# A layer on one core: the transfer queue from the end of attention on, in the program's order

## Chip, core and metric

The kernel runs on one core of a Trainium2 chip. The metric is the device time of one execution in microseconds (us); the profile is one more execution, taken apart by the hardware profiler. A core has TensorE (PE), VectorE (DVE), ScalarE (ACT), GpSimd (POOL) and SyncE (SP). SP computes nothing: it issues the DMA transfers, one after the other, and waits for semaphores in between.

## The reference

One encoder layer on 512 tokens of width 1024, in float32.

```python
h = rmsnorm(x, g_mix_pre)
aq, ..., gate_logits = split(h @ w_in)
ya = dsa_attention(...) @ w_up_a             # sparse attention, 8 heads
yb = stick_breaking_attention(...) @ w_up_b  # 8 heads
yc = memory_attention(...) @ w_up_c          # 4 heads on 256 memory tokens
gates = sigmoid(gate_logits + b_gate)        # three gates of (512, 1024)
merged = gates[0] * ya + gates[1] * yb + gates[2] * yc
x = x + rmsnorm(merged @ w_out, g_mix_post)
h = rmsnorm(x, g_ffn_pre)
gu = h @ w_ffn_in                            # 1024 -> 2 * 2816
x = x + rmsnorm((silu(gu[:2816]) * gu[2816:]) @ w_ffn_out, g_ffn_post)
```

## The kernel before

Every float32 product is made of three passes on TensorE. Each operand is split into a rounded high part, made by ACT (`split`, line 76), and the low rest, made by DVE (line 77); the passes are high x high, high x low and low x high. So each weight tile of 128 x 1024 floats (512 KB) goes through four steps: SP loads it (`load`, line 97), ACT casts it, DVE subtracts, TensorE uses it.

Buffers have tags, each with a fixed number. `load` puts weights into `wraw` (3 buffers) and, from the end of attention on, into `lraw` (2 buffers) for every second load. The split of a `wraw` tile goes to `wh` and `wl` (2 each), that of an `lraw` tile to a wide tile `w2` (4). `act` (22 buffers) holds nearly all else: queries, keys, merged activations, gains, and some raw weights. `h` (8) holds the normed activations, `fin` (4) the residual stream.

The order of instructions: TensorE's is the program's everywhere, by a region of `manual_schedule` around the whole layer. DVE, ACT and POOL have such regions in two places only (the first norm, and the end of mix_out). Elsewhere a scheduler orders ACT, DVE, POOL and SP ahead of time, along an estimated clock: it takes what is ready in its own plan, and prefers what stands earlier in the program. An instruction that first writes a tile can only be placed when the plan has a buffer for the tile, and the tiles of one tag are handed out in the program's order. Within a region an engine's instructions keep the order of the program; where they fall among instructions from outside the region stays the scheduler's. When the program runs, each engine goes through its list in order and waits for semaphores only.

`run` (from line 267) is the layer. What matters here comes after the attention branches:

- **merge(1)** (line 697) runs in TensorE's gaps of the last attention branch and then alone: for each of 8 column blocks a gate (weights of w_in) and an up-projection (w_up_b, 12 matmuls of 512 columns). TensorE's result is multiplied with the gate on DVE (line 726), added to `acc` on POOL (line 727), and split into a pair mT[j] of tag `act` on ACT and DVE (line 730).
- **mix_out** (line 800): the gain of the norm (`grow`, line 734, tag `act`), the four x rows (line 354, tag `fin`), then `tok_pair` (line 737) twice, for tokens 0 to 255 and 256 to 511: mT times w_out, row block after row block (12 matmuls each, line 751). In the first pass the weights of ffn blocks 0 and 1 are loaded on the way, raw into `act`; the second pass keeps four of the eight row blocks from the first.
- **ffn** (line 1001): ffn blocks 0 to 2 as plain products, and blocks 3 to 21 (`seven`, `left_sides`) by Strassen's scheme, seven products a block. A block loads its gate half into `wraw` and its up half into `lraw`.
- **ffn_out** (line 1048): the gain of the last norm (tag `h`), ten row blocks of w_ffn_out as plain products, and the other twelve by Strassen, with the products in the order 5, 1, 2, 6, 3, 7, 4. Their raw weights are read in `units51` and `unit`; some are summed by accumulating transfers from POOL (line 1070). Then the norm and the stores (line 792).

In program order the transfers of mix_out are: gain; x rows 0 to 3; w_out 0 (`wraw`), 1 (`lraw`); both halves of ffn block 0 (`act`); w_out 2, 3; both halves of block 1; w_out 4 to 7; in the second pass w_out 0, 1, both halves of block 2, w_out 2, 3. Even rows go to `wraw`, odd ones to `lraw`.

Of the kernel before, what the change touches and what calls it, by code (L numbers as in the profile page):

```python
# [48 lines left out]
class Layer:  # L49
# [217 lines left out]
    def run(self):  # L267
        w_in, w_kv = self.a["w_in"], self.a["w_mem_kv"]
        late = ExitStack()
        att = ExitStack()  # L270
        self.att = att.enter_context(self.tc.tile_pool(name="att", bufs=1))
        with self.tc.manual_schedule(engines={mybir.EngineType.PE}):
            self.setup()
            memT, mk, mv, cq = [], {}, {}, {}
            self.index_keys(cq)
            xs = [self.load_rows(self.a["mem"], t) for t in range(2)]
            for x in xs:
                self.norm_in(x)

            self.iq = {}  # L280
            iqs = lambda js: self.feat_tiles(w_in[:, C_IQ:C_IQ + 512], self.hT, self.iq, js, T - P, P,
                                             lambda ps: self.evac_q(ps[:, 0:T - P], T - P), self.w_iq)
            cqs = lambda js: self.feat_tiles(w_in[:, C_CQ:C_CQ + 512], self.hT, cq, js)
            mks = lambda js: self.feat_tiles(w_kv[:, 0:512], memT, mk, js, n=M)
            mvs = self.tok_tiles(w_kv[:, 512:1024], memT, (0, 1), mv)
            memTs = self.mem_T(xs, memT)
            iq = self.add(iqs(range(4)))
            kv = self.add(cqs((1,)), self.mix(memTs, cqs((2,)), 2), mks(range(4)), cqs((3,)), mvs)
            self.drain(iq)
            self.scores()  # L290
            self.drain(kv)
            a, aq = self.qkv(C_AQ, C_AK, C_AV)
            self.branch_c(cq, mk, mv)
            self.acc = {}
            self.add(self.merge(2, self.outC, "w_up_c"))
            self.drain(aq)
            self.select()
            self.fill(FM)
            b, bq = self.qkv(C_BQ, C_BK, C_BV)
            self.branch_a(*a)  # L300
            self.drain(bq)
            self.add(self.merge(0, self.outA, "w_up_a"))
            self.outB = []
            self.add(self.merge(1, self.outB, "w_up_b"))
            self.branch_b(*b)
            self.drain()
            att.close()
            self.late = late.enter_context(self.tc.tile_pool(name="late", bufs=1))
            self.mix_out()
            self.ffn()  # L310
        late.close()

    def setup(self):
# [687 lines left out]
    def ffn(self):  # L1001
# [31 lines left out]
        for j, u in enumerate(first[1:], 1):  # L1033
            run(products(*u, 1))
            self.gated(u[0], out(j))
# [199 lines left out]
```

## Time and profile before

| | us |
|---|---|
| median of 3 runs | 908.74 |
| lowest and highest | 907.76, 911.09 |
| profiled execution | 906.76 |
| its span, first to last instruction | 905.0 |

Busy shares of the span: TensorE 97%, DVE 75%, ACT 53%, POOL 13%. The span falls into attention with merge(1) (to about 503 us), mix_out (to about 543), the ffn blocks (to about 777) and ffn_out (to the end). A busy TensorE means matmuls in a row; the idle time in between is where a wait shows.

### The profile page before, as it was taken

Reading aid. Unit: us, or ns where it says so; the run is one execution under the profiler, and the core shown is the slowest. Engines: PE = TensorE matmul, PEld = TensorE weight load, DVE = VectorE, ACT = ScalarE, POOL = GpSimd, SP = SyncE. Lnnn points to the kernel's source line nnn. Section 1 sums busy time; section 2 is a strip of 40 time slices with the busy share of each in tenths; the row PEclk is TensorE's granted clock in tenths of the full one; section 3 lists DMA queues with packets and bytes.
Section 4 is the critical chain, followed back from the end, with each engine's and each line's share of the span. In section 5 each row is a group of like instructions: output and inputs, shape, how many; then the busy total and the mean of one; then the engine's idle time right before and its main releaser. Section 6 shows DMA issues by size and latency. Waiting matters only on the chain.

```text
span 905.0 us, 13554 instructions
## 1 busy us (share of the span) xinstructions
PE 881.1 (97%) x5110; PEld 773.9 (86%) x5110; DVE 681.5 (75%) x1174; ACT 476.0 (53%) x830; POOL 120.4 (13%) x157
## 2 busy tenths in 40 slices
PE   8999999999999999999999999999999999999995
PEld 7888888888888888888788888999999999887884
DVE  6589999953598976777563579688888887862886
ACT  6464675332666666665453454355555555542452
POOL 2000000020032303443222101500000000000101
PEclk9999999999999999999999999999999999999998
DMA  6523543443354433222384723113434334672622
GB/s 204 170 85 119 166 115 94 127 129 111 101 160 119 128 82 93 70 59 59 116 253 132 237 79 105 48 44 98 116 95 116 96 115 121 189 215 81 176 34 93
DMA packets 134341, 107.47 MB, mean 119 GB/s; under 512 B 4844, under 2 KB 115484, under 8 KB 134276
## 3 DMA queue, kind: packets, MB, share of 16 engines
q1 hardware_dynamic: 132052, 102.41, 38.5%
q0 software_dynamic: 1632, 3.15, 2.2%
q8 instruction: 40, 0.66, 0.3%
q10 hardware_dynamic: 592, 1.05, 0.3%
q14 instruction: 25, 0.20, 0.1%
HBM read 100.02 MB, written 2.12 MB: 113 GB/s over the span
## 4 chain that ended last, share of the span: by engine, by line
PE 77%; DVE 12%; issue 4%; DMA 3%; ACT 2%; POOL 1%; POOLq 0%; DVEq 0%; ACTq 0%
PE bank L88 21%; PE bank L87 21%; PE bank L89 21%; DVE wl L77 4%; PE bank L751 3%; PE bank L551 2%; PE bank L566 1%; PE bank L181 1%; PE bank L180 1%; PE bank L211 1%; DMA lraw<-in_w_ffn_out_dram 1%; PE bank L213 1%; PE bank L212 1%; DVE act L77 1%; DVE e L638 1%
## 5 line engine op out<-in xcount | busy, mean ns | idle before, releaser
L77 DVE TENSOR_TENSOR wl<-wraw,wh 128x1024 fp32r<-128x1024 f32 (+1 forms) x107 | 122.4, 1146 | 66.7 <-ACT wh L76 66.4
L76 ACT CAST wh<-wraw 128x1024 fp32r<-128x1024 f32 (+1 forms) x107 | 102.0, 955 | 111.5 <-PE bank L88 75.6
L87 PE MATMUL bank<-h,wh 128*128 128x512 f32 (+1 forms) x376 | 148.8, 396 | 0.0
L89 PE MATMUL bank<-h,wl 128*128 128x512 f32 (+1 forms) x376 | 145.3, 386 | 1.0 <-DVE wl L77 0.9
L88 PE MATMUL bank<-h,wh 128*128 128x512 f32 (+1 forms) x376 | 145.0, 386 | 0.0
L89 PEld LDWEIGHTS bank<-h,wl 128*128 128x128 f32 x376 | 70.6, 188 | 15.8 <-DVE wl L77 1.7
L87 PEld LDWEIGHTS bank<-h,wh 128*128 128x128 f32 x376 | 70.9, 189 | 11.7 <-issue 0.2
L88 PEld LDWEIGHTS bank<-h,wh 128*128 128x128 f32 x376 | 70.8, 188 | 11.5
L87 PE MATMUL bank<-act,wh 128*128 128x256 f32 (+1 forms) x204 | 69.2, 339 | 1.2 <-DVE s L976 1.2
L88 PE MATMUL bank<-act,wh 128*128 128x256 f32 (+1 forms) x204 | 68.0, 333 | 0.0
L89 PE MATMUL bank<-act,w 128*128 128x256 f32 x228 | 64.1, 281 | 0.0
L87 PE MATMUL bank<-h,w 128*128 128x256 f32 x228 | 64.1, 281 | 0.0
L88 PE MATMUL bank<-h,w 128*128 128x256 f32 x228 | 64.1, 281 | 0.0
L89 PE MATMUL bank<-h,w 128*128 128x256 f32 x228 | 64.1, 281 | 0.0
L87 PE MATMUL bank<-act,w 128*128 128x256 f32 x228 | 64.1, 281 | 0.0
L88 PE MATMUL bank<-act,w 128*128 128x256 f32 x228 | 64.1, 281 | 0.0
L615 POOL TENSOR_TENSOR p<-toep,score 128x128 f32<-128x128 f32 (+3 forms) x32 | 30.5, 967 | 200.2 <-DVE score L524 102.9
L77 DVE TENSOR_TENSOR act<-act 128x512 fp32r<-128x512 f32 (+1 forms) x47 | 36.0, 778 | 22.3 <-ACT act L76 22.2
L76 ACT CAST act<-act 128x512 fp32r<-128x512 f32 (+1 forms) x47 | 31.6, 692 | 32.6 <-POOL act L727 13.9
L77 DVE TENSOR_TENSOR w<-wl,w 128x1024 fp32r<-128x1024 f32 x38 | 46.3, 1218 | 1.5 <-ACT w L76 1.0
L87 PE MATMUL bank<-h,act 128*128 128x256 f32 (+2 forms) x152 | 46.8, 308 | 0.0
L88 PE MATMUL bank<-h,act 128*128 128x256 f32 (+2 forms) x152 | 45.7, 301 | 1.1 <-DVE h L81 1.1
(224 smaller groups left out, 2306.4 us busy)
## 6 DMA issues: line engine op xcount, KB each, us to landing
wraw<-in_w_in_dram SPq DMA_DIRECT2D x64, 512.0 KB, 3.7
lraw<-in_w_ffn_in_dram SPq DMA_DIRECT2D x20, 512.0 KB, 3.9
wraw<-in_w_ffn_in_dram SPq DMA_DIRECT2D x20, 512.0 KB, 3.7
wraw<-in_w_ffn_out_dram SPq DMA_DIRECT2D x13, 512.0 KB, 4.5
lraw<-in_w_ffn_out_dram SPq DMA_DIRECT2D x12, 512.0 KB, 3.6
wraw<-in_w_mem_kv_dram SPq DMA_DIRECT2D x8, 512.0 KB, 3.9
lraw<-in_w_out_dram SPq DMA_DIRECT2D x6, 512.0 KB, 6.1
wraw<-in_w_out_dram SPq DMA_DIRECT2D x6, 512.0 KB, 4.6
```

The source lines that it names most:

```text
L76: self.nc.scalar.copy(hi, src)
L77: (eng or self.nc.vector).tensor_tensor(lo, src, hi.bitcast(F32), op=OP.subtract)
L87: self.nc.tensor.matmul(out, lhsT=sh, rhs=mh, start=first and i == 0, stop=False, **kw)
L88: self.nc.tensor.matmul(out, lhsT=sh, rhs=ml, start=False, stop=False, **kw)
L89: self.nc.tensor.matmul(out, lhsT=sl, rhs=mh, start=False, stop=last and i == n - 1, **kw)
L180: self.nc.tensor.matmul(out, lhsT=x, rhs=y[:, 0:n], start=True, stop=False)
L181: self.nc.tensor.matmul(out, lhsT=x, rhs=y[:, T:T + n], start=False, stop=True)
L211: self.nc.tensor.matmul(ps, lhsT=ah[:, s], rhs=wh[:, k2], start=st, stop=False)
L212: self.nc.tensor.matmul(ps, lhsT=ah[:, s], rhs=wl[:, k2], start=False, stop=False)
L551: self.nc.tensor.transpose(ps[:, c:c + P], p[i][:, j * P:(j + 1) * P], self.ident)
L615: nc.gpsimd.tensor_tensor(s, toep[0][:, 0:n][:, ::-1], self.mask[i], op=OP.add)
L751: self.nc.tensor.matmul(ps[c], lhsT=st_[:, s], rhs=mv_[:, 0, c * 512:(c + 1) * 512], start=f and k == order[0], stop=l and k == order[-1])
```

## The change

`run` wraps its last two calls in a region in which SP, too, issues in the order of the program:

```diff
             self.late = late.enter_context(self.tc.tile_pool(name="late", bufs=1))
-            self.mix_out()
-            self.ffn()
+            with self.tc.manual_schedule(engines={mybir.EngineType.SP}):
+                self.mix_out()
+                self.ffn()
         late.close()
```

`ffn` calls `ffn_out`, so all transfers from the gain of mix_out to the last store on SP are in the region. The loads of merge(1) are not. The transfers that ACT and POOL issue stay as they are.

## Rows read from the trace of the kernel before

**Rows 1.** The page, part 1: busy us (share of the span) x instructions, by engine.

```profile
PE 881.1 (97%) x5110; PEld 773.9 (86%) x5110; DVE 681.5 (75%) x1174; ACT 476.0 (53%) x830; POOL 120.4 (13%) x157
```

**Rows 2.** Busy time by stretch: length, engines, TensorE's granted clock, DMA share, GB/s.

```profile
450.00:460.00 10.00, 10.00 (x46) 8.28 (x45) 4.43 (x5) 3.79 (x7) 1.67 (x1) 1.00 0.98 355
505.00:525.00 20.00, 20.00 (x89) 16.28 (x88) 10.41 (x10) 8.32 (x10) 2.14 (x1) 1.00 0.83 262
530.00:575.00 45.00, 42.11 (x278) 37.78 (x277) 37.15 (x74) 22.24 (x48) 8.83 (x10) 1.00 0.36 106
760.00:780.00 20.00, 18.75 (x157) 18.50 (x156) 16.57 (x26) 13.01 (x20) 1.37 (x1) 1.00 0.49 144
800.00:830.00 30.00, 28.52 (x123) 22.72 (x122) 16.55 (x19) 13.12 (x17) 1.21 (x1) 1.00 0.59 176
```

**Rows 3.** TensorE's timeline, end of merge(1) and last matmul: start, us, instruction.

```profile
503.13 0.39 PE L89 MATMUL bank<-act,wl 128*128 128x512 f32 x1
...
504.09 0.73 PE L751 MATMUL bank<-wl,act 128*128 128x512 f32 x2
...
894.00 0.40 PE L89 MATMUL bank<-w,act 128*128 128x512 f32 x1
```

**Rows 4.** SP's timeline, end of attention to mix_out (x2, x3: two, three transfers).

```profile
447.75 1.29 SPq L354 DMA_DIRECT2D fin<-in_x_dram  x3
...
454.31 0.90 SPq L97 DMA_DIRECT2D lraw<-in_w_out_dram  x2
...
483.91 2.29 SPq L97 DMA_DIRECT2D wraw<-in_w_up_b_dram  x2
492.07 12.32 SPq L97 DMA_DIRECT2D wraw<-in_w_out_dram  x4
504.44 0.43 SPq L734 DMA_DIRECT2D act<-in_g_mix_post_dram  x1
```

**Rows 5.** Timelines of DVE and of ACT around the end of merge(1).

```profile
490.81 1.23 DVE L77 TENSOR_TENSOR wl<-wraw,wh 128x1024 fp32r<-128x1024 f32 x1 [2.49 <-ACT wh L76]
492.68 0.69 DVE L726 TENSOR_TENSOR gate<-bank,gate 128x512 f32<-128x512 f32 x1 [0.64 <-PE bank L89]
...
504.56 0.68 DVE L726 TENSOR_TENSOR gate<-bank,gate 128x512 f32<-128x512 f32 x1
...
495.14 0.62 ACT L76 CAST act<-act 128x512 fp32r<-128x512 f32 x1 [2.07 <-POOL act L727]
...
500.61 1.05 ACT L76 CAST wh<-wraw 128x1024 fp32r<-128x1024 f32 x1 [1.51 <-PE bank L88]
...
507.56 0.62 ACT L76 CAST act<-act 128x512 fp32r<-128x512 f32 x1 [3.00 <-POOL act L727]
508.08 1.05 ACT L76 CAST wh<-wraw 128x1024 fp32r<-128x1024 f32 x1
```

**Rows 6.** Busy time by stretch behind the last matmul; the clock is the seventh figure.

```profile
897.00:898.00 1.00, 0.00 (x0) 0.00 (x0) 0.16 (x1) 0.92 (x3) 0.00 (x0) 0.83 0.96 367
898.00:900.00 2.00, 0.00 (x0) 0.00 (x0) 1.52 (x5) 0.42 (x2) 0.93 (x1) 0.50 0.01 2
```

**Rows 7.** SP's timeline at the end of the ffn blocks.

```profile
742.30 0.34 SPq L97 DMA_DIRECT2D wraw<-in_w_ffn_out_dram  x1
...
762.14 0.34 SPq L97 DMA_DIRECT2D wraw<-in_w_ffn_out_dram  x1
765.88 0.33 SPq L734 DMA_DIRECT2D h<-in_g_ffn_post_dram  x1
766.30 6.62 SPq L97 DMA_DIRECT2D lraw<-in_w_ffn_out_dram  x2
```

**Rows 8.** Timelines of DVE and of ACT at the start of ffn_out.

```profile
771.34 1.22 DVE L1135 TENSOR_TENSOR act<-wraw,lraw 128x1024 f32<-128x1024 f32 x1 [0.66 <-DMA lraw<-in_w_ffn_out_dram]
...
799.59 1.23 DVE L1135 TENSOR_TENSOR act<-wraw,lraw 128x1024 f32<-128x1024 f32 x1 [4.95 <-DMA lraw<-in_w_ffn_out_dram]
...
774.66 1.05 ACT L76 CAST wh<-wraw 128x1024 fp32r<-128x1024 f32 x1
```

## The prediction

> **What bounds the kernel now.** I read the page first, then busy time by stretch, then SP's timeline, then TensorE, VectorE (DVE), ScalarE (ACT) and GpSimd (POOL) around the place where the change begins. TensorE is busy for 97% of the span [rows 1]; in the part that the change reaches it is full in 450 to 460 and in 505 to 525, and misses 2.89 us in 530 to 575, 1.25 us in 760 to 780 and 1.48 us in 800 to 830 [rows 2]. Add the tail behind the last matmul (it starts at 894.00 and takes 0.40, [rows 3]; the span is 905.0): some 5.6 us of holes and 10.6 us of tail are all that a better order could win. Transfers don't bound it: 0.83 of the DMA engines' time in 505 to 525, and 0.98 in 450 to 460, with TensorE full in both [rows 2]. What can cost is a hole put into TensorE's stream, whose order is fixed by hand.
>
> **What SP does now.** At the end of attention the scheduler runs ahead of the program. The x rows leave at 447.75, and while merge(1) (gates and up-projection, ends at 503.5) still runs, the odd rows of w_out leave from 454.31 on, through the `lraw` buffers that nothing else wants [rows 4]. The even rows wait for a `wraw` buffer from merge(1): four of them from 492.07 on. The first transfer of mix_out in the program, the gain row, leaves at 504.44, behind 14 later ones [rows 4]. It has nothing to wait for in the data: it goes into an `act` buffer. Tiles of one tag are handed out in the program's order, and the `act` tiles just ahead of it are the eight pairs mT that merge(1) writes. So in the scheduler's plan the gain can't get its buffer before ACT takes up the split of mT[7], though at run time a buffer has been free for long. That is the hinge of this case.
>
> **The change, part by part.** It adds and removes no instruction. From mix_out on it chains SP's list: gain, four x rows, w_out 0, 1, two halves of ffn block 0, w_out 2, 3, block 1, w_out 4 to 7, and so on; in ffn_out the gain of the last norm, and then w_ffn_out.
>
> 1. *The plan.* The gain is now the head of the chain, and all 14 transfers that the plan used to place ahead of it (four x rows, nine w_out rows, one half of ffn block 2) are behind it. In the plan the first w_out row therefore starts after the split of mT[7] is begun, and its conversion (ACT `wh`, then DVE `wl`) must stand behind that split in ACT's queue. Before, the conversion of w_out 0 stood at 500.61, ahead of the splits of mT[6] and of mT[7] (507.56) [rows 5].
>
> 2. *The run.* SP only follows semaphores, and there it is not late: behind the last up-projection load (by 483.91 + 2.29 = 486.2, [rows 4]) the gain and the x rows go out at once, w_out 0 goes when its `wraw` buffer is free, at about 492.07 as now, and w_out 1 just behind it. The five early transfers are 2.6 MB; at the 355 GB/s of [rows 2] that is 7.4 us, done by about 494, and w_out 0 lands by 498. Nobody uses it before 503.5. If that cover were gone, the price would be the rest of those 7.4 us.
>
> 3. *The hole.* The data are there, but ACT's queue now says mT[7] first. The last matmul of merge(1) starts at 503.13 and takes 0.39 [rows 3]: it ends at 503.52. DVE has the low half of mT[6] to do first (0.6), so its product with the gate starts at about 504.2. From that product to the split on ACT it is 2.46 us two tiles earlier (492.68 to 495.14, the POOL add in it) and 3.00 for the last tile (504.56 to 507.56) [rows 5]; DVE is emptier then, so I take 2.5: 506.7. The next conversion starts 0.52 later (507.56 to 508.08) and takes 1.05 (the one at 500.61): 508.3. There TensorE gets its first two matmuls of mix_out; the third needs `wl`, 1.23 us on DVE (490.81) [rows 5]: 509.5. That matmul starts at 504.09 now [rows 3]. Sum: 509.5 - 504.1 = **+5.4 us**. Ends: DVE's product directly at 503.56, 2.46 and the same three steps, 508.8, +4.7; DVE and POOL no quicker than now, 507.56 + 0.52 + 1.05 + 1.23 = 510.4, +6.3.
>
> 4. *What comes behind it.* Four odd rows that were converted during merge(1) are converted now while TensorE uses them: 4 x 1.23 us more on DVE, on top of 10.41 of 20 us in 505 to 525 [rows 2], makes 15.3; ACT 8.32 + 4 x 1.05 = 12.5. A row is ready every 1.23 us and TensorE needs 12 matmuls for one, 12 x 0.23 = 2.8 us (89 matmuls in 20 us, [rows 2]), so it is hidden after the first; without that cover each row would cost up to 1.2 us. SP itself is held: the last half of block 1 goes into a buffer that TensorE frees half way through merge(1)'s last 12 matmuls (12 x 0.23 before 503.5, so about 502), and w_out 4 to 7 are queued behind it, so w_out 4 leaves some 3 us later than now. It is wanted at about 520. w_out 5 and 7 wait for `lraw` buffers until w_out 1 and 3 are converted, at about 511 and 515, and are wanted at 523 and 528. Cost: 0.
>
> 5. *The clock.* After the last matmul of the kernel (ends at 894.40) the granted clock is 0.83 in 897 to 898 and 0.50 from 898 on [rows 6]: 1.2 GHz in place of 2.4 after an idle time shorter than the hole of 4.8 us in step 3. No row shows a clock that comes back. Bounds: 0, if it doesn't fall, and one step of 12 matmuls at half speed, 2.8 us. I take +1.0, nearer to none since the hole is barely longer than what it took to fall. The Trainium skill, "TensorE: Matmul & The Clock Gate" (the part on the HAM clock gate), says that low is the resting state and that only sustained matmul activity releases it. The fall at the end of this trace agrees with it; by that rule the hole would cost the slow step too, which is the second rival below.
>
> 6. *The ffn blocks.* The halves of a block now alternate strictly, where the plan had the `wraw` half one block ahead. The `lraw` half decides how far ahead a block can be loaded, it has two buffers, and it leaves when it does now; the `wraw` half then leaves just behind it, a block or more ahead of its use. Cost: 0.
>
> 7. *ffn_out.* Its gain wants an `h` buffer, free at 765.88; w_ffn_out 0 leaves at 742.30 today, and the fourth at 762.14 [rows 7]. All of them go behind the gain now. The first is converted only at 774.66 (it lacks a `wh` buffer until then, [rows 8]); leaving at 766.2, with the 5.0 us that the load at 766.30 takes to its use at 771.34 [rows 7, 8], it is there at about 771: 3 us to spare. The pair for the first Strassen sum comes some 5 us later, and DVE has waits that take this up (4.95 us at 799.59, [rows 8]). Cost 0; bounds -1.25 (the hole in 760 to 780 closes) to +5 (that wait of 4.95 lands on TensorE).
>
> 8. *The end.* Three reads of T[7] wait for `act` buffers that the first of the seven products (order 5, 1, 2, 6, 3, 7, 4) frees, and six reads that ran earlier now follow them. The first three of the six are wanted for the fifth product, the others for the seventh, and a product is 36 matmuls of 0.23, 8.3 us: 0, bounds -1 to +1. The stores keep their order.
>
> Sum: 5.4 + 1.0 = +6.4 us. The profiled execution took 906.76 us (span 905.0 and 1.8 around it), which is 2.0 under the median of 908.74; against its own time that is 913.2, and against the median 915.1.
>
> **The rivals.** *No hole*: the change doesn't do what I read into it, that is, ACT's queue keeps w_out 0 ahead of mT[7]. For it: the data are early at run time. Against it: the gain's place at 504.44, 57 us behind its successors [rows 4]. It gives 908.7. *A slow restart*: the clock falls in the hole and stays at 1.2 GHz for two steps, 5.5 us in place of 1.0: 908.7 + 5.4 + 5.5 = 919.7. *Starved ffn_out*: the list begins 24 us later (742.30 to 766.2), and the wait of DVE for a transfer at 799.59 grows to one of TensorE: 5 to 6 us more, 921. For it: 1.48 us are lost right there already; against it: the 3 us to spare in step 7 and the buffers that hold the list back anyway. *Faster*: loads in order of use close the three holes (2.89 + 1.25 + 1.48 = 5.6 us): 903.1. It decides only if there is no hole at the start of mix_out, and the holes in 530 to 575 lie in the norms between TensorE and DVE, not at a transfer.
>
> **How the numbers follow.** Forecast 0.62, no hole 0.14, slow restart 0.10, starved ffn_out 0.08, faster 0.06. The forecast's own range is +4.7 - 1.0 to +6.3 + 2.8: 912.4 to 917.8. The range has to reach the slow restart and most of the no-hole and starved cases: 909 to 921. A measurement of this kernel can tell about 0.5% (4.5 us) from no change: faster takes the last rival but for its weaker half, 0.05; same the no-hole case and the low end of the forecast, 0.18; slower 0.77.
>
> **What would show it.** In the profile after: SP's gain and x rows behind the last up-projection load, at about 486; no `lraw` load of w_out before 492; on ACT the split of mT[7] ahead of the first `wh` of w_out; a hole on TensorE of 4 to 5 us from 503.5 on, ended by ACT `wh`, and a shorter one ended by DVE `wl`; a granted clock under 1.00 in 505 to 515 if step 5 counts. The first w_ffn_out load at or behind the gain of the last norm, and holes after 760 of the size that they have now. I am wrong if TensorE runs through at 503 to 510, or if the time is lost where transfers are waited for.

## The result, and the profile after

The changed kernel takes 919.75 us (median of 4 executions, 918.88 to 920.12), the kernel before 908.25 beside it (4 executions). The ratio is 1.0124, with a 95% interval of 1.0109 to 1.0139: 11.5 us slower. The forecast was 915.1, +6.4. The sign and the first place were right; the size was not, and two more places had been put at nothing.

The profiled execution took 920.12 us, its span is 918.3, so the span grew by 13.3; that is more than 11.5 because the profiled execution before (906.76) lies under its median and this one over its own. All numbers below are places in these two spans; line numbers of the changed kernel are higher by one. First the page, part 1 (busy us, share, instructions), which answers to [rows 1]:

```profile
PE 884.7 (96%) x5110; PEld 775.8 (84%) x5110; DVE 678.6 (74%) x1174; ACT 475.5 (52%) x830; POOL 119.7 (13%) x157
```

The work is the same, instruction by instruction. TensorE is busy 3.6 us longer for the same 5110 matmuls, so some of them ran slower; the rest of the growth is idle time. Where it is idle, the view of TensorE's waits from 500 us on shows (engine and line, what was waited for, total us, times, longest):

```profile
PE bank L752 <- ACT wh L76: 4.5, 1, 4.5
PE bank L87 <- DVE s L977: 2.9, 1, 2.9
```

Before, the first of these waits did not exist and the second was 1.25 us.

**First place, the start of mix_out.** SP's timeline (start, us, instruction), to hold beside [rows 4]:

```profile
484.09 2.29 SPq L97 DMA_DIRECT2D wraw<-in_w_up_b_dram  x2
486.44 0.50 SPq L735 DMA_DIRECT2D act<-in_g_mix_post_dram  x1
487.02 2.00 SPq L355 DMA_DIRECT2D fin<-in_x_dram  x4
492.25 0.33 SPq L97 DMA_DIRECT2D wraw<-in_w_out_dram  x1
492.62 0.43 SPq L97 DMA_DIRECT2D lraw<-in_w_out_dram  x1
```

SP is early: gain and x rows right behind the last up-projection load, w_out 0 at 492.25 as before. The hole is made elsewhere. TensorE, then ACT, then DVE, to hold beside [rows 3, 5]:

```profile
503.31 0.39 PE L89 MATMUL bank<-act,wl 128*128 128x512 f32 x1
508.17 1.22 PE L752 MATMUL bank<-wh,act 128*128 128x512 f32 x2 [4.47 <-ACT wh L76]
509.43 1.22 PE L752 MATMUL bank<-wl,act 128*128 128x512 f32 x2
...
513.79 0.63 PE L752 MATMUL bank<-w,act 128*128 128x512 f32 x2
...
506.55 0.62 ACT L76 CAST act<-act 128x512 fp32r<-128x512 f32 x1 [2.76 <-POOL act L728]
507.07 1.04 ACT L76 CAST wh<-wraw 128x1024 fp32r<-128x1024 f32 x1
...
504.43 0.68 DVE L727 TENSOR_TENSOR gate<-bank,gate 128x512 f32<-128x512 f32 x1
...
508.14 1.23 DVE L77 TENSOR_TENSOR wl<-wraw,wh 128x1024 fp32r<-128x1024 f32 x1 [0.25 <-ACT wh L76]
```

ACT splits mT[7] at 506.55 and converts w_out 0 only behind it, at 507.07; before, that conversion stood at 500.61. The third matmul of mix_out starts at 509.43, before at 504.09. The matmuls of w_out 1, which start at 513.79 here, started before at

```profile
506.49 2.93 PE L751 MATMUL bank<-w,act 128*128 128x512 f32 x12
```

The next view shows the granted clock (third figure from the right; the second is TensorE's busy time):

```profile
506.00:507.00 1.00, 0.00 (x0) 0.00 (x0) 0.00 (x0) 0.45 (x1) 0.52 (x1) 0.94 1.23 321
507.00:513.00 6.00, 4.80 (x10) 3.31 (x11) 5.55 (x6) 6.00 (x8) 0.00 (x0) 0.50 0.44 142
513.00:514.00 1.00, 1.00 (x4) 0.84 (x3) 1.00 (x2) 1.00 (x2) 0.00 (x0) 0.65 0.99 356
514.00:515.00 1.00, 1.00 (x6) 0.80 (x5) 1.00 (x2) 1.00 (x2) 0.00 (x0) 1.00 0.84 344
```

The clock falls to 0.50 (1.2 in place of 2.4 GHz) at about 506.9, while TensorE is idle, and is back at about 513.7. The first w_out row is used at half speed: from the third matmul to the group with w_out 1 it is 4.36 us, before 2.40. The Trainium skill, "TensorE: Matmul & The Clock Gate" (the HAM clock gate), says that low is the resting state and matmul activity releases it; these rows agree: it is back after TensorE has worked from 508.17 on.

**Second place, the start of ffn_out.** TensorE, ACT, DVE and SP in turn:

```profile
786.42 0.39 PE L87 MATMUL bank<-act,wh 128*128 128x256 f32 x1 [2.94 <-DVE s L977]
...
782.26 1.05 ACT L76 CAST h<-wraw 128x1024 fp32r<-128x1024 f32 x1 [2.58 <-DMA wraw<-in_w_ffn_out_dram]
783.22 1.03 ACT L76 CAST wh<-wraw 128x1024 fp32r<-128x1024 f32 x1
784.94 0.63 ACT L974 ACTIVATE silu<-silu 128x512 f32<-128x512 f32 x1 [0.69 <-DVE silu L973]
...
783.35 1.23 DVE L77 TENSOR_TENSOR h<-wraw,h 128x1024 fp32r<-128x1024 f32 x1 [2.23 <-ACT h L76]
784.49 0.42 DVE L973 TENSOR_TENSOR silu<-bank,s 128x256 f32<-128x256 f32 x1
...
785.95 0.42 DVE L977 TENSOR_TENSOR s<-bank,s 128x256 f32<-128x256 f32 x1
...
772.58 0.34 SPq L735 DMA_DIRECT2D h<-in_g_ffn_post_dram  x1
772.97 0.42 SPq L97 DMA_DIRECT2D wraw<-in_w_ffn_out_dram  x1
```

The gain of the last norm leaves at 772.58 and all of w_ffn_out behind it. ACT comes to a conversion of w_ffn_out (into `h`) and stands there 2.58 us for its transfer; DVE stands 2.23 us for ACT. Behind these stands what TensorE waits for: the sum into `s` (line 977), which frees the PSUM bank (the place of TensorE's result) that the last product needs.

The tile is the first of Strassen's product 1 (`right(1, 0, ...)` in `units51`): third of w_ffn_out in the program, so third in the chain. It is one of five loads that leave within 2.6 us (SP's timeline has it at 773.92), and could be used only 8.3 us later, at 782.26. ACT had this conversion ahead of the last silu in the kernel before too, with its load there; what ended its wait then was TensorE:

```profile
766.19 1.05 ACT L76 CAST h<-wraw 128x1024 fp32r<-128x1024 f32 x1 [1.50 <-PE bank L89]
...
776.54 0.63 ACT L973 ACTIVATE silu<-silu 128x512 f32<-128x512 f32 x1 [0.83 <-DVE silu L972]
```

So it is not the order on ACT that is new here, but the late load in it. Behind this hole the clock was at 0.50 too, from about 786.8 to 790.2:

```profile
787.00:790.00 3.00, 3.00 (x13) 2.81 (x13) 2.32 (x5) 1.93 (x2) 0.00 (x0) 0.50 0.46 128
```

**Third place, the tail.** SP, DVE and TensorE:

```profile
851.40 3.11 SPq L97 DMA_DIRECT2D act<-in_w_ffn_out_dram  x3
854.62 0.41 SPq L97 DMA_DIRECT2D wraw<-in_w_ffn_out_dram  x1
...
869.51 0.37 SPq L97 DMA_DIRECT2D lraw<-in_w_ffn_out_dram  x1
...
904.48 0.68 DVE L1184 TENSOR_TENSOR act<-bank,act 128x512 f32<-128x512 f32 x1
...
909.66 0.68 DVE L1184 TENSOR_TENSOR act<-bank,act 128x512 f32<-128x512 f32 x1
...
904.08 0.40 PE L89 MATMUL bank<-w,act 128*128 128x512 f32 x1
```

The three reads of T[7] wait for `act` buffers until 851.40, and the last six reads now stand behind them (854.62 to 869.51). Before, five of the six had left by 840, ahead of T[7] at 842.10, and the last at 845.71. Their conversions reach DVE late; from 881.86 on it works almost without a break, the norms of the first two blocks of tokens come later too (to 904.0, before to 889.5), and the sum that opens the norm of the third block runs at 904.48, behind the start of TensorE's last matmul. Before it ran 2.9 us ahead of it. T[7] and that sum in the kernel before:

```profile
842.10 3.11 SPq L97 DMA_DIRECT2D act<-in_w_ffn_out_dram  x3
...
891.12 0.68 DVE L1183 TENSOR_TENSOR act<-bank,act 128x512 f32<-128x512 f32 x1
```

From one such sum to the next it is 5.2 us (904.48 to 909.66). So two of these steps follow the last matmul, where before 1.9 us of the first were left behind it (894.40 to 896.30) and the whole second: 3.3 us more.

**The account**, by where the same instruction starts in the two spans:

| where | lag, us | added there |
|---|---|---|
| last matmul of merge(1): 503.13, 503.31 | 0.18 | 0.18 |
| third matmul of mix_out: 504.09, 509.43 | 5.34 | 5.16, the hole |
| first group with w_out 1: 506.49, 513.79 | 7.30 | 1.96, the clock |
| end of the ffn blocks: 776.78, 783.48 | 6.70 | -0.60, in the norms |
| next matmul: 778.03, 786.42 | 8.39 | 1.69, second hole |
| clock at 1.00 again: 780.73, 790.64 | 9.91 | 1.52, the clock |
| last matmul: 894.00, 904.08 | 10.08 | 0.17 |
| end of the span: 905.0, 918.3 | 13.30 | 3.22, the tail |

### The profile page after: what moved, and what is told of

Read it like the earlier page. It is cut to its first block, busy times and chain, and to the rows that moved or that the text cites. A ratio compares the mean times of both kernels' runs of the same rounds, so it can differ in the third digit from the quotient of the medians.

```text
span 918.3 us, 13534 instructions
## 1 busy us (share of the span) xinstructions
PE 884.7 (96%) x5110; PEld 775.8 (84%) x5110; DVE 678.6 (74%) x1174; ACT 475.5 (52%) x830; POOL 119.7 (13%) x157
## 3 DMA queue, kind: packets, MB, share of 16 engines
HBM read 100.02 MB, written 2.12 MB: 111 GB/s over the span
## 4 chain that ended last, share of the span: by engine, by line
PE 79%; DVE 11%; issue 4%; DMA 2%; ACT 2%; POOL 2%; SPq 0%; POOLq 0%; DVEq 0%; ACTq 0%
PE bank L87 22%; PE bank L88 22%; PE bank L89 22%; PE bank L752 3%; DVE wl L77 3%; PE bank L552 2%; PE bank L567 1%; PE bank L181 1%; PE bank L180 1%; PE bank L211 1%; PE bank L213 1%; PE bank L212 1%; DVE e L639 1%; POOL rs L247 1%; DMA wraw<-in_w_ffn_out_dram 1%
## 5 line engine op out<-in xcount | busy, mean ns | idle before, releaser
L87 PEld LDWEIGHTS bank<-h,wh 128*128 128x128 f32 x376 | 70.9, 189 | 11.6 <-issue 0.2
L88 PEld LDWEIGHTS bank<-h,wh 128*128 128x128 f32 x376 | 70.8, 188 | 11.5
L89 PE MATMUL bank<-act,wl 128*128 128x512 f32 (+1 forms) x128 | 46.5, 363 | 0.0
```

The lines of the kernel that those rows point to most:

```text
L87: self.nc.tensor.matmul(out, lhsT=sh, rhs=mh, start=first and i == 0, stop=False, **kw)
L88: self.nc.tensor.matmul(out, lhsT=sh, rhs=ml, start=False, stop=False, **kw)
L89: self.nc.tensor.matmul(out, lhsT=sl, rhs=mh, start=False, stop=last and i == n - 1, **kw)
```

## Experiments

The theory: three places, each with its own cause: the first from the order that a chain on SP forces on the plan, the other two from loads that are late because of what stands ahead of them in the chain. The rivals: one cause that the later losses follow from; the program's order as such; slow matmuls for another reason than the clock.

**One part alone.** First the region over ffn alone, then over mix_out alone:

```diff
-            with self.tc.manual_schedule(engines={mybir.EngineType.SP}):
-                self.mix_out()
-                self.ffn()
+            self.mix_out()
+            self.ffn()
...
+        chain = ExitStack()
+        chain.enter_context(self.tc.manual_schedule(engines={mybir.EngineType.SP}))
         self.gated(pss, out(0))
...
         self.ffn_out(fT)
+        chain.close()
```

> SP's list is in the program's order only from the end of the norms on (ffn blocks and ffn_out); mix_out keeps the scheduler's order. Theory (the loss is a sum of places that don't depend on each other: hole of 5.2 and slow clock of 2.0 at the start of mix_out, hole of 1.7 and slow clock of 1.5 at the start of ffn_out, 3.2 in the tail): here the first two are gone and the others stay, some 6.5 us over before (914 to 915.5), and TensorE starts on mix_out at about 504 as before. Rival (what is lost in ffn_out is a consequence of the late start of mix_out, or of where the gain of mix_out stands): within 1.5 us of before.

Measured: 913.07 beside 908.09 (ratio 1.0060, 1.0039 to 1.0080), 5.0 us, a little under what was expected.

```profile
779.57 0.39 PE L87 MATMUL bank<-act,wh 128*128 128x256 f32 x1 [2.46 <-DVE s L976]
```

The second hole is there (2.46 us) and the long tail (895.52 to 909.8, 14.3 us; before 11.0). In this trace the clock stayed at 1.00 behind this hole, which is the missing 1.5 us. It is the fastest of the four executions (mean granted clock 0.995); the others have 0.988 to 0.992, so some of them hold slow clock that no trace shows.

> SP's list is in the program's order only over mix_out up to its norms; the ffn blocks and ffn_out keep the scheduler's order. Theory of separate places: a hole of about 4.5 us at 503.5 ended by ACT wh, the clock at 0.50 behind it, and nothing lost behind 780: some 6.6 us over before (914 to 915.5), and this run and the one with the region over ffn alone add up to the loss of the change, 11 to 13 us. Rival (the two parts act on each other: the queue of ffn pulls the buffers of mix_out): the sum of the two differs from the loss of the change by over 2 us.

Here the region ends ahead of mix_out's ordered tail. Measured: 915.88 (1.0079, 1.0059 to 1.0100), 7.8 us, a little over what was expected. The hole of 4.47 us and the slow clock are there; at the start of ffn_out TensorE waits 2.03 us, 0.8 more than before, and the tail is 11.2 us. The trace also has a clock of 0.50 from 555.0 to 558.4, behind a wait of 2.14 us in the norms; the kernel before waits 2.24 us there and its clock stays. The two parts add up to 12.8 us, the whole is 11.5: separate places, within the spread of the runs.

**The head of the chain.** The first gain is asked for ahead of the region:

```diff
+            self.gp = self.grow("g_mix_post", "act")
             with self.tc.manual_schedule(engines={mybir.EngineType.SP}):
...
-        gp = self.grow("g_mix_post", "act")
+        gp = self.gp
```

> As the change, but the first gain row is asked for ahead of the region, so that it isn't the head of SP's chain; all else in program order. Theory (the hole comes from the head of the chain: its act buffer is handed out behind the split of mT[7], so everything chained behind it is planned behind it too): x rows and w_out 0 are planned earlier, w_out 0 is converted ahead of mT[7]'s split, no hole over 1 us at 503.5, clock 1.00 through 505 to 515: 7 us under the changed kernel, 912 to 913.5. Rival (order itself: in program order the loads come too late or too close together, whatever the head): the hole stays within 1 us of 4.5, time within 1 us of the changed kernel.

Measured: 914.22, 5.5 us under the changed kernel where 7 were expected. ACT, then TensorE:

```profile
500.65 1.05 ACT L76 CAST wh<-wraw 128x1024 fp32r<-128x1024 f32 x1 [1.32 <-PE bank L88]
...
506.74 2.52 ACT L76 CAST act<-act 128x512 fp32r<-128x512 f32 x3 [3.09 <-POOL act L729]
...
510.26 0.73 PE L753 MATMUL bank<-wh,act 128*128 128x512 f32 x2 [0.80 <-ACT wh L76]
511.90 0.50 PE L753 MATMUL bank<-wl,act 128*128 128x512 f32 x1 [0.91 <-DVE wl L77]
```

w_out 0 is converted at 500.65, ahead of mT[7]'s split (in the group at 506.74), as before; the hole of 4.5 us is gone and the clock is at 1.00 there. What stays is 1.7 us of waits: the third row (510.26, 511.90) is converted behind that split now. That is the part of the 7 us that did not come. The wait of 2.39 us at the start of ffn_out, with the clock at 0.50 behind it, and the tail of 14.2 us are still there. So the hole is what the head of the chain had made, not program order itself.

**The buffer.** The gain stays the head of the chain, in a buffer of its own:

```diff
-    BUFS = dict(h=8, act=22, wraw=3, wh=2, wl=2, lraw=2, pt=3, fin=4)
+    BUFS = dict(h=8, act=21, wraw=3, wh=2, wl=2, lraw=2, pt=3, fin=4, gain=1)
...
-        gp = self.grow("g_mix_post", "act")
+        gp = self.grow("g_mix_post", "gain")
```

> As the change, with the first gain still the head of SP's chain, but in a buffer of its own; act has 21 buffers in place of 22, which may cost a little anywhere. Theory (what holds the chain back in the plan is the act buffer that is handed out only behind the last pair mT): with no such buffer to wait for, w_out 0 is converted ahead of mT[7]'s split and the hole of 4.5 us is gone, as with the gain ahead of the region: 912 to 915, what the 21 buffers cost included. Rival (being behind a head in program order is what counts, whatever its buffer): the hole stays within 1 us of 4.5, some 919 to 921.

The place answers: no hole, with the same two short waits behind it. ACT and TensorE:

```profile
502.61 1.05 ACT L76 CAST wh<-wraw 128x1024 fp32r<-128x1024 f32 x1 [1.39 <-PE bank L88]
...
505.13 0.39 PE L89 MATMUL bank<-act,wl 128*128 128x512 f32 x1
505.36 0.61 PE L752 MATMUL bank<-wh,act 128*128 128x512 f32 x2
```

w_out 0 is converted at 502.61, ahead of mT[7]'s split, which is in the group of ACT that starts at 508.71. So being the head alone does not make the hole; it is the `act` buffer, handed out behind the eight pairs mT. One thing stays argued: `act` has 21 buffers here, and no run has 21 with the gain still among them. The time, 918.06, is no proof of it: merge(1) ends 1.8 us later with 21 buffers, and TensorE loses 4.5 us ahead of 870, where ACT stands at conversions into `h` for three late loads in turn (4.60, 1.45 and 1.94 us), and the clock falls behind that.

**The last gain.** It is asked for where the reads of the third product follow, late in ffn_out:

```diff
-        gp = self.grow("g_ffn_post", "h")
...
         s1 = copied(px)
+        gp = self.grow("g_ffn_post", "h")
         more(3)
```

> As the change, but the gain row of the last norm is asked for where it is first needed less early, behind the ten plain row blocks of ffn_out's weights, so that the loads of w_ffn_out aren't chained behind its h buffer. Theory (the hole at the start of ffn_out is the late start of w_ffn_out's list, held by that gain): the first w_ffn_out loads leave tens of us earlier, the DVE wait of 2.9 us at 786 and the slow clock behind it are gone, 1.7 to 3.2 us under the changed kernel (916.5 to 918); the tail stays 13.8. Rival (the hole is the order of the reads themselves or of the buffers wraw and lraw): within 1 us of the changed kernel and the hole stays.

Measured: 918.42, only 1.3 us under the changed kernel. The mechanism is as expected, the gain smaller:

```profile
753.17 0.57 SPq L97 DMA_DIRECT2D wraw<-in_w_ffn_out_dram  x1
...
783.21 0.39 PE L87 MATMUL bank<-act,wh 128*128 128x256 f32 x1 [0.57 <-DVE s L977]
```

The first load leaves at 753.17 in place of 772.97, the hole is 0.57 in place of 2.94 us, and no slow clock follows. So it is the place of that gain in the chain that made the load late. Some of it comes back as waits of 0.7 and 0.5 us for ACT and 0.9 for a `wl` that were not there or shorter. The tail stays, 14.2 us. Behind the first hole the clock of this trace was low for half as long as in the changed kernel (508.5 to 511.9), which no edit here accounts for.

**T[7].** Its three reads are taken out of the chain:

```diff
+        self.chain.close()
         for i in range(n):
             T[7, i] = read(0, 1, i, "act")
             plus(T[7, i], 1, 1, i)
+        self.chain.enter_context(self.tc.manual_schedule(engines={mybir.EngineType.SP}))
```

> As the change, but the three reads of T[7] in ffn_out are taken out of SP's chain: the reads chained behind them no longer wait for the act buffers that T[7] needs. Theory (the tail of 14.2 us in place of 11.0 is the late start of six reads behind T[7], which pushes DVE's sums into the last product): those reads leave before T[7] as in the kernel before, DVE has a gap ahead of the last product, the tail is 11 us and the time 3.2 us under the changed kernel (916 to 917). Rival (the tail is longer because the whole of ffn_out starts later or because the last transfers collide): the tail stays at 14 us.

Measured: 919.89, no gain. Yet five of the six reads leave ahead of T[7] again (826.31 to 852.88, T[7] from 854.99), and the tail is 10.2 us (906.89 to 917.1). Most of the 4 us are lost again ahead of it. ACT and TensorE:

```profile
833.17 1.04 ACT L76 CAST h<-wraw 128x1024 fp32r<-128x1024 f32 x1 [6.26 <-DMA wraw<-in_w_ffn_out_dram]
834.12 1.04 ACT L76 CAST wh<-lraw 128x1024 fp32r<-128x1024 f32 x1
...
835.21 0.65 PE L87 MATMUL bank<-wh,act 128*128 128x512 f32 x1 [3.28 <-ACT wh L76]
...
906.89 0.40 PE L89 MATMUL bank<-w,act 128*128 128x512 f32 x1
```

It is the second place's mechanism again: in ACT's list a conversion whose load is late stands ahead of the one that TensorE wants, and the clock falls behind the hole. Here this order is new: the changed kernel has no conversion into `h` at that place. The tail's cause is shown: it is 14.2 to 14.3 us in six traces with T[7] in the chain (12.8 in the seventh, whose TensorE lost 4.5 us late), and 10.2 to 11.6 in the four with T[7] out of it. Taken away alone, it gave nothing back.

**Both of ffn_out's repairs.**

> As the change, with the last gain asked for later and T[7]'s reads out of SP's chain, both at once; the first gain stays the head of the chain. Theory (the hole of 3.3 us at 832 that came with freeing T[7] alone is ACT in its planned order standing at a conversion whose load is late because the whole list of w_ffn_out is late; with the list early it is at most 1.3 us, as with all three taken back): hole and slow clock at 503 to 515 stay, nothing else is lost, tail 10 to 11.2: 914 to 916.5, within 1.5 us of the run that has program order over mix_out alone. Rival (the two repairs get in each other's way, or a hole at 832 is the price of freeing T[7]): 917 or more, with a hole over 2.5 us behind 800.

Measured: 917.38 (914.22 to 918.30). The traced execution is the fastest of the four: 914.22, waits of 0.57 at 783 and 1.30 at 830, tail 11.5 us. The holes are as small as the theory said, but the clock is at 0.50 from 832.6 to 836.0 behind the waits of 1.30 and 0.76 us, the tail is a little longer than expected, and the median is 1 us above. What the other three lost isn't in a trace.

**All three taken back.**

> As the change, with three things taken back: the first gain asked for ahead of the region, the last gain asked for later, T[7]'s reads out of the chain. Theory (these three are the whole loss; program order itself costs next to nothing): hole, both slow-clock stretches and the long tail are gone; what stays are some 1.7 us of short waits for w_out rows at 509 to 512, as in the run with the first gain ahead alone: 908 to 911, within 3 us of the kernel before. Rival (something else of the order costs too): over 912.

Measured: 912.89 as the median of ten, from 908.12 to 915.87. The traced one is the fastest, 908.12: no hole at 503, short waits of 0.8 and 0.9 at 510 to 512, 0.6 at 779, 1.3 at 826, tail 11.1 us, clock at 1.00 to the last matmul. That is what was expected, but the median is 2 us over the upper end, as the rival had it: 4.9 us over the kernel before (ratio 1.0050, 1.0029 to 1.0071). The ten differ by their mean granted clock: 0.997 at 908.12, 0.992 to 0.993 at 912.4 to 912.9, 0.989 to 0.990 at 915.6 to 915.9. A step of 0.008 of some 910 us is 7.3 us; the times differ by 7.8. So the other executions hold slow clock that this trace doesn't show; behind which waits, is open.

**ffn alone, mended.** The region over ffn alone with both of ffn_out's repairs:

> Program order on SP only from the end of the norms on, with the last gain asked for later and T[7]'s reads out of the chain; mix_out has the scheduler's order. Theory (nothing is left of the loss, and the loads of ffn_out in order of use may take back the waits of 1.25 us at 777 and 1.48 us at 800 to 830): 906 to 908.5, at or up to 2 us under the kernel before. Rival (order of use does nothing for these waits, which are DVE's and ACT's own): within 1 us of before; or a new wait is made, over 910.

Measured: 911.16 (1.0038, 1.0023 to 1.0054), slower than before. The wait at 777 is 1.0 in place of 1.25 us, those in 800 to 830 grew from 1.48 to 1.90: ACT stood 4.13 us for the load of a conversion into `h` ahead of the `wh` that TensorE wanted. The clock fell twice in this trace: behind the wait of 2.12 us in the norms, ahead of the region, and behind 1.15 and 0.76 us at 826. Order of use wins nothing there. No kernel tried here is faster than the one before.

**The clock alone.** Idle transposes of the identity fill the hole:

```diff
+        idle = self.bank()
+        for _ in range(21):
+            nc.tensor.transpose(idle[:, 0:P], self.ident, self.ident)
         gp = self.grow("g_mix_post", "act")
```

> As the change, plus 21 transposes of the identity on TensorE at the start of mix_out that nobody reads, so that TensorE isn't idle through the whole hole. Theory (the slow first step behind the hole is the granted clock that falls in it): the hole for the data stays (the first matmul of mix_out at about 508), the clock is 1.00 over 505 to 515, 2 us under the changed kernel (917 to 918.5). Rival (the step is slow because its weights come late, and the clock is only a bystander): time and the start of the second step unchanged, within 0.7 us.

Measured: 917.95, 1.8 us under the changed kernel. But 2.18 us of the hole stayed idle and the clock fell all the same, for about half as long (0.50 over 509 to 512, 1.00 from 513). So it was run again with 40:

> As the run with 21 idle transposes at the start of mix_out, with 40 of them: at the 0.117 us each that the 21 took (2.46 us) they last from 503.5 to about 508.2 and fill the hole, in which 21 left 2.2 us idle and the clock still fell, for half as long. Theory (the slow steps behind the hole are the clock, and only idle time brings it down): clock 1.00 all through 503 to 515, the first conversions and the first four matmuls at the same times as in the changed kernel, its w_out 1 (the group of 12 matmuls, at 513.79 there) at about 511.8; 917 to 918 at the median, 2 us under the changed kernel. Rival (a clock that falls for its own reasons, or matmuls that wait for weights): the group of 12 at 513 or later.

Measured: 917.71. TensorE's timeline:

```profile
503.63 4.53 PE L805 MATMUL bank<-ident 128*128 128x128 f32 x40
508.27 0.73 PE L752 MATMUL bank<-wh,act 128*128 128x512 f32 x2
...
511.93 2.93 PE L752 MATMUL bank<-w,act 128*128 128x512 f32 x12
```

and the clock by stretch:

```profile
503.00:509.00 6.00, 5.89 (x46) 5.04 (x44) 2.74 (x4) 2.97 (x4) 1.49 (x2) 1.00 1.03 337
509.00:512.00 3.00, 2.47 (x12) 2.06 (x12) 3.00 (x4) 3.00 (x5) 0.00 (x0) 1.00 0.17 33
```

The data come when they came before (508.27), the clock stays at 1.00, and the group with w_out 1 starts 1.86 us earlier, at 511.93. The slow first row was the clock: of the 1.96 us, 1.86 came back with it.

## Why the prediction was right, and where it was not

**Steps 1 and 2 (plan and run): right.** The split of mT[7] stands ahead of w_out 0's conversion, SP is early all the same, no `lraw` load of w_out leaves ahead of 492. That the gain's `act` buffer does it, was argued from the code then; the runs with the gain ahead of the region and in a buffer of its own show it (the second with 21 `act` buffers in place of 22).

**Step 3 (hole, +5.4): right.** Forecast 508.3 and 509.5, measured 508.17 and 509.43, added 5.16. Each term held: DVE's product 504.43 (504.2), split 506.55 (506.7), conversion 507.07 (507.2).

**Step 4 (behind the hole, 0): right.** No later wait for a w_out row. Its cover is thin: when the first row is freed, the third costs 1.7 us.

**Step 5 (clock, +1.0): too small.** It cost 1.96, within the bounds of 0 to 2.8. The choice "nearer to none since the hole is barely longer than what it took to fall" was wrong: once it had fallen, TensorE worked from 508.17 to about 513.7 at half speed, and only what the wait for `wl` (to 509.4) hid was free.

**Step 6 (ffn blocks, 0): right.** The lag shrinks from 7.30 to 6.70 between the first rows of w_out and the end of the blocks, all of it at one wait in the norms (2.24 us before, 1.63 now), and TensorE waits for no load there.

**Step 7 (ffn_out, 0): wrong, 1.69 and 1.52 for the clock.** For the first load the sum held: its conversion (783.22) waited for no transfer. What failed is the choice of the conversion that needs a load first. The step read "The first is converted only at 774.66", but ACT had taken up a tile of w_ffn_out at 766.19 already, into `h`, for product 1. Of that tile's lateness the step priced only DVE's sum of the pair, not ACT's conversion nor the low half that DVE makes of it. Its load is the third of five that leave together, and could be used only at 782.26; ACT stood 2.58 us for it and DVE 2.23 for ACT, with the last block's silu and the sum that frees TensorE's bank behind them. The upper bound, 5 us, named another wait (799.59), which did not reach TensorE.

**Step 8 (end, 0, bounds -1 to +1): wrong, 3.22.** The step asked whether the six reads come in time for TensorE's fifth and seventh products. Nearly so: TensorE lost 0.17 us. The overlap that it left out is DVE's other work: the late conversions push back the norms of the first two blocks of tokens, and these push the third block's first sum from 2.9 us ahead of the last matmul to 0.4 behind its start.

**The rivals.** "No hole" and "faster" fell. "Slow restart" (919.7) gave nearly the right number by the wrong sum: two steps at half speed were not seen. "Starved ffn_out" (921) had the place and not the wait: the late list hurt through ACT's conversion of the third load. The range of 909 to 921 held the time by luck as far as the sum goes: it reached that far for the rivals, and none of them is what came. The forecast's own range of 912.4 to 917.8 did not hold it. Its upper end adds the bounds of steps 3 and 5 alone; step 7's +5 and step 8's +1 are in no sum, and these two steps cost 6.4 of the 13.3 us.

## What to carry to other kernels

Ordering one engine's queue by hand also changes what the scheduler plans for the others: ask of the chain's head when its buffer is handed out, and then read which conversions move ahead of which on the engines that work through their lists in order. When a whole list of loads moves, look for the instruction that takes up any of them first, not for the use of the first load. A cost of a moved transfer is not only "does it land before its use", but "who stands in the queue behind the instruction that waits for it", and what else that engine has to do when the work comes late. A repair that closes one such wait can open the next one, so price it by the end of the span and not by the wait.

## What the runs showed of the hardware

The length of a hole does not by itself decide whether the clock falls. Behind 4.47 us it fell in all five traces with that hole (changed kernel, region over mix_out, last gain late, T[7] free, both of ffn_out's repairs), in two of them for about half as long as in the others. Shorter holes went either way:

| where | the clock fell behind | it stayed behind |
|---|---|---|
| start of ffn_out, us | 2.94, 2.39, 1.98 | 2.56, 2.46, 2.19, 2.03, 1.88 |
| in the norms, us | 2.14, 2.12 | 2.39, 2.24 (the kernel before) |
| two waits close together, us | 1.30 and 0.76, 1.15 and 0.76 | 1.28 and 0.76 |

A small wait can so cost more than its own length, in one trace and not in another.

Idle work was enough to hold it here: 40 transposes in 4.53 us, with the clock at 1.00 throughout; one trace shows it. The Trainium skill, "TensorE: Matmul & The Clock Gate" (Part 4, PE-mode transpose), says that the full clock does not engage for transposes. Here, where the trace lists them as matmuls by the identity in float32, they kept a full clock that was already there; whether they would raise a low one, no run shows.
